# A two-block transformer kernel: output rows cleared earlier, the expert gate moved to VectorE, expert places reordered, and the closing sum made on TensorE

## The chip, the cores and the metric

The kernel runs on one core of a Trainium2 chip. A core has five engines, each with an instruction stream of its own that it works through in order: TensorE (PE, with its weight loads as PEld), VectorE (DVE), ScalarE (ACT), GpSimd (POOL) and SyncE (SP, which here only issues DMA transfers). Engines wait for one another by semaphores. The metric is the device time of one execution in microseconds (us), lower is better. The time before is 3085.83 us, the median of three runs.

## The reference

The input is 1024 tokens of width 1024, all in float32. Two blocks follow one another; the second is where most of the change lies.

```
x = first_block(x, p, ...)      # forgetting attention (16 heads), layer norm,
                                # conv-GELU FFN (2816), layer norm, gate
# second_block:
mod = silu(c) @ w_ada + b_ada
shift1, scale1, gate1, shift2, scale2, gate2 = split(mod, 6)
h   = rmsnorm(x, norm1_w) * (1 + scale1) + shift1
mix = concat(retention(h), gated_delta_rule(h)) @ w_out
x   = x + gate1 * mix
h2  = rmsnorm(x, norm2_w) * (1 + scale2) + shift2
# MoE: top-1 of 4 groups, then top-2 of the 8 experts in it; 32 experts, width 512
hid = silu(xs @ w1[e]) * (xs @ w3[e])         # xs: tokens of expert e
ys  = hid @ w2[e] * gate
x   = x + gate2 * segment_sum(ys, tok)
return rmsnorm(x, final_norm_w)
```

## The kernel before

**Precision.** A float32 product is made as three faster products. `split` (L83 to L91) writes a rounded copy `hi` (on ACT at L86, or on POOL by `pool_copy`, L80) and the rest `lo` = source − `hi` on DVE (L91); the three matmuls then stand at L108 to L110, or at L1581 for an expert's output.

**Loads.** All weight loads go through SP's one queue. `load_stage` (L150 to L154) fills one of two buffers `wst`. In the expert stage `fetch` (L1237 to L1246) takes the next of 29 buffers of 512 KB in turn (their names in the trace are `r`, `Bh`, `Bl`, `x`), so that it can run at most 29 blocks ahead of their use. An expert's weights are 12 blocks: four of `w1`, four of `w3`, four of `w2`.

**Experts.** Tokens are sorted by the number that each expert got, and the 32 experts stand in *places* of four kinds: `s` (places 0 to 2, one tile of 128 rows), `T` (3 to 6, two tiles), `M` (7 to 15, one tile of 96 or 128 rows) and `L` (16 to 31, 64 rows or fewer). `L` places use the float32 weights as they are, with no split; the other kinds split each block into a pair of parts, and `ring` (L481) holds five such pairs. `ORDER_OF` (L41) says in which order the kinds are worked. For each place POOL gathers the token rows (L1473), PE turns them (L148), `expert` (L1508 to L1590) computes, and at its end the output `y` leaves PSUM: ACT copies two halves into a `wst` buffer (L1587), POOL multiplies by the row `gate2` (`g2_row`, L1588), and POOL scatters the rows to `y_d` in DRAM by an indirect DMA (L1589). The last two places are kept on the chip by `keep` (L1592 to L1599) in the tile `both`.

**y_d.** Each token has two rows in `y_d`, one for each of its experts. Rows that no scatter writes must be zero, so POOL clears `y_d` at the start of the FFN of block 1 with two DMAs of 4 MB (L580 to L582).

**Tail.** When the experts are done, the eight tiles of 128 rows of x (`R`) and both halves of `y_d` (`Y`) are loaded (L1674, L1675). `add_rows` (L1688 to L1696) sums them: POOL adds the first `Y` to `R`, PE adds the second (through the matrix `ident`) to the kept rows (through the 0/1 matrix `oh`), DVE adds that, ACT sums squares. `scales` (L1698 to L1701) computes the norm, `finish` (L1703 to L1709) applies it and writes the output: odd tiles by ACT and POOL (L1705, L1706), even ones by DVE (L1708). `FIN` (L46) is the order of these steps (`a` add, `c` scales, `f` finish).

The order of instructions on each engine is fixed when the kernel is built, by a scheduler of the framework that works from the code's order and its own estimates.

Of the kernel before, what the change touches and what calls it, by code (L numbers as in the profile page):

```python
# [21 lines left out]
T = 1024  # L22
# [17 lines left out]

ORDER_OF = "sss" + "LLT" * 4 + "MMM" + "ML" * 6 + "LL"  # L41

GROUP = 3

RET, OUT_LAG, R_LAG = 2, 3, 2
FIN, FIN_POOL = "aaaacaaaaffffcffff", (1, 3, 5, 7)  # L46

# [78 lines left out]
def tile_kernel(ctx: ExitStack, tc: tile.TileContext, a: dict, out: bass.AP):  # L126
# [35 lines left out]
    with ph:  # L162
# [18 lines left out]
        def x_tile(t):  # L181
            xt = load_stage(x[t * 128:(t + 1) * 128, :])
            for g in range(2):
# [5 lines left out]
                split(nc, ps, xh[dst], xl[dst])  # L189

        w_in = a["attn_w_in"][0]

# [52 lines left out]
        def project(hp, begin=False):  # L245

            for i in range(2):
                kd[hp, i] = st_p.tile([128, T], F32R, name="kd")
                k66[hp, i] = st_p.tile([66, T], F32R, name="k66")
            w = load_w_cols(D + hp * 128)  # L250
            for hf in range(2):
                if hf == begin:
                    for i in range(2):
                        nc.gpsimd.dma_start(k66[hp, i][64:66, :], c_d[:, 2 * hp + i, :])
                s = slice(hf * 512, hf * 512 + 512)
                for ps in proj(w, hf):
                    yield
                for i in range(2):
                    src = ps[64 * i:64 * i + 64, :]
                    kk = kd[hp, i]  # L260
                    nc.scalar.activation(kk[0:64, s], src, AF.Copy)
                    nc.vector.tensor_tensor(k66[hp, i][0:64, s], src, kk[0:64, s], op=OP.subtract)  # L262
                    pool_copy(nc, kk[64:128, s], kk[0:64, s])
                if begin and hf == 0:
                    yield
# [263 lines left out]


    ada_d = dram.tile([6, D], F32, name="ada_d")
    ones_m = consts.tile([128, 128], F32, name="ones_m")
# [5 lines left out]
    def ada(pl):  # L538
        for j in range(6):
# [10 lines left out]
            for c in range(2):  # L550
                cs = slice(c * 512, (c + 1) * 512)
                ps = ps_g.tile([128, 512], F32, name="g")
                mm(ps, ones_m, acc[:, cs], start=True, stop=True)
                nc.vector.tensor_tensor(o_[:, cs], ps[0:1, :], b[0:1, cs], op=OP.add)
                if j in (1, 4):
# [20 lines left out]
    with tc.tile_pool(name="ffn", bufs=2, **TW) as fp:  # L576

        y_d = dram.tile([2 * T, D], F32, name="y_d")
        zero = fp.tile([128, 256], F32, name="zero", bufs=1)
        nc.gpsimd.memset(zero, 0.0)  # L580
        for k in range(2):
            nc.gpsimd.dma_start(y_d[k * T:(k + 1) * T, :].rearrange("(p t) (c f) -> p (t c) f", p=128, f=256),  # L582
                                zero[:, None, :].to_broadcast([128, 32, 256]))
        w_up = a["ffn_w_up"][0]
# [663 lines left out]
    def blocks(w1_, w3_, w2_, small):  # L1248

        up = [(w, k2) for w in (w1_, w3_) for k2 in range(4)]  # L1250
        if small:
            up = [(w, k2) for k2 in range(4) for w in (w1_, w3_)]
        return ([w[k2 * 256:(k2 + 1) * 256, :].rearrange("(k p) f -> p k f", p=128) for w, k2 in up] +
                [w2_[k * 128:(k + 1) * 128, :] for k in range(4)])
# [5 lines left out]
    with tc.tile_pool(name="mix", bufs=2, **TW) as pl:  # L1260
        wr = pl.tile([128, NK, 36], F32, name="wr", bufs=1)
        nc.sync.dma_start(wr[:, :, 0:4], a["w_group_2"][0].rearrange("(k p) f -> p k f", p=128))
        nc.sync.dma_start(wr[:, :, 4:36], a["w_expert_2"][0].rearrange("(k p) f -> p k f", p=128))
        br = pl.tile([128, 36], F32, name="br", bufs=1)
# [14 lines left out]
        def begin(t, c):  # L1279
# [5 lines left out]
            cs = slice(c * 512, (c + 1) * 512)  # L1285
            V.tensor_tensor(h2[t][:, cs], R[t][:, cs], A2[:, cs], op=OP.mult)
            nc.scalar.activation(junk, R[t][:, cs], AF.Square, scale=1.0 / 32, accum_out=ss[t][:, c:c + 1])
# [220 lines left out]
    def expert(whole, tiles, small=False, final=None, pair=None):  # L1508
# [60 lines left out]
        for n_, hT_, (_, _, dst) in zip(ns, hT, tiles):  # L1569
# [16 lines left out]
            for c in range(2):  # L1586
                nc.scalar.activation(ys[0:n_, c * 512:(c + 1) * 512], py[c], AF.Copy)  # L1587
            nc.gpsimd.tensor_tensor(ys[0:n_, :], ys[0:n_, :], g2_row[0:n_, :], op=OP.mult)  # L1588
            nc.gpsimd.indirect_dma_start(out=y_d[:, :], out_offset=bass.IndirectOffsetOnAxis(ap=dst, axis=0),  # L1589
# [82 lines left out]
    for _ in cur:  # L1672
        pass
    R = [fetch(x4_d[t * 128:(t + 1) * 128, :]) for t in range(NT)]  # L1674
    Y = [[fetch(y_d[k * T + t * 128:k * T + (t + 1) * 128, :]) for k in range(2)] for t in range(NT)]  # L1675
    fn = row(mo, a["final_norm_w_2"][None, :], "xTh", 2)
# [11 lines left out]
    def add_rows(t):  # L1688
        nc.gpsimd.tensor_tensor(R[t], R[t], Y[t][0], op=OP.add)
        for c in range(2):  # L1690
            cs = slice(c * 512, (c + 1) * 512)
            ps = ps_h.tile([128, 512], F32, name="h")
            mm(ps, ident, Y[t][1][:, cs], start=True, stop=False)
            mm(ps, oh[:, t * 128:(t + 1) * 128], both[:, cs], start=False, stop=True)
# [8 lines left out]
    def finish(t):  # L1703
        if t in FIN_POOL:
            nc.scalar.activation(R[t], R[t], AF.Copy, scale=y[:, t:t + 1])  # L1705
            nc.gpsimd.tensor_tensor(R[t], R[t], fn, op=OP.mult)  # L1706
        else:
            nc.vector.scalar_tensor_tensor(R[t], R[t], y[:, t:t + 1], fn, op0=OP.mult, op1=OP.mult)  # L1708
        nc.sync.dma_start(out[0, t * 128:(t + 1) * 128, :], R[t])  # L1709

    added = scaled = ended = 0
    for step in FIN:
# [3 lines left out]
        elif step == "c":  # L1716
            scales(scaled, added - scaled)
            scaled = added
        else:
# [30 lines left out]
```

## Time and profile before

| | |
|---|---|
| median of three runs | 3085.83 us (3080.3 to 3089.42) |
| the profiled execution | 3084.05 us, span 3082.2 us |
| TensorE's granted clock, mean over the span | 0.971 |
| PE / PEld / DVE / ACT / POOL busy | 93% / 71% / 57% / 33% / 21% |
| traffic | 440.97 MB, mean 143 GB/s |
| attention, from the start to about | 600 us |
| FFN of block 1, from about | 710 us |
| expert stage (32 places) | 2414 to 3033 us |
| tail | 3033 to 3082.2 us |

The span is what the profiler saw from the first to the last instruction; the execution's own time is 1.85 us longer. PE's 93% is a mean over stages: what a change in one stage is worth depends on what PE waits for in that stage.

### The profile page before, as it was taken

The page shows a single profiled execution, that of the slowest core. Times are in us where ns is not written, and L with a number is a line of the kernel's source. Part 1 is how long each engine was busy: PE and PEld are TensorE (multiplying, and loading weights), DVE is VectorE, ACT ScalarE, POOL GpSimd, SP SyncE. Part 2 cuts the span into 40 slices and gives each one's busy share as a digit, 9 for nine tenths or more (in the row PEclk, how much of TensorE's full clock was granted, in tenths as well). Part 3 has the DMA queues.
Part 4 walks back from the last instruction along what each step waited for, and adds up shares of the span by engine and source line. Part 5 has one row for each costly group of instructions (what it writes and reads, how often), then busy time and mean ns, then how long its engine had stood idle before and what let it go on. Part 6 is the DMA issues. An engine that isn't in the chain of part 4 may idle for free. (4 is left out here: it accounts for less than half of the span.)

```text
span 3082.2 us, 38291 instructions
## 1 busy us (share of the span) xinstructions
PE 2876.8 (93%) x13931; PEld 2175.1 (71%) x13931; DVE 1763.1 (57%) x3065; ACT 1015.0 (33%) x1773; POOL 652.7 (21%) x636
## 2 busy tenths in 40 slices
PE   7999999897999999999997999999996799999995
PEld 5777777676787877877776888888775555465542
DVE  4666666565565554555956545543568743367655
ACT  4555555512121212122224322232222333244432
POOL 2333332100000000000120022211223334444444
PEclk9999999998999999999998999999998799999998
DMA  3110111516232232332235422222556698988997
GB/s 100 34 32 29 35 36 39 185 53 194 66 116 82 82 97 69 95 96 76 102 77 96 90 72 69 78 77 71 187 162 235 234 342 315 335 306 312 382 378 286
DMA packets 276922, 440.97 MB, mean 143 GB/s; under 512 B 42698, under 2 KB 138058, under 8 KB 276604
## 3 DMA queue, kind: packets, MB, share of 16 engines
q1 hardware_dynamic: 267068, 413.28, 41.1%
q0 software_dynamic: 9664, 25.23, 2.4%
q8 instruction: 111, 1.82, 0.2%
q14 instruction: 79, 0.65, 0.1%
HBM read 382.00 MB, written 64.12 MB: 145 GB/s over the span
## 5 line engine op out<-in xcount | busy, mean ns | idle before, releaser
L108 PE MATMUL g<-Bh,hi 128*128 128x512 f32 x896 | 358.7, 401 | 6.1 <-ACT hi L86 4.9
L110 PE MATMUL g<-Bh,lo 128*128 128x512 f32 x896 | 357.2, 399 | 0.8 <-DVE lo L91 0.8
L109 PE MATMUL g<-Bl,hi 128*128 128x512 f32 x896 | 356.5, 398 | 1.2 <-DVE Bl L91 1.2
L108 PE MATMUL g<-hi,Bh 128*128 128x512 f32 x704 | 283.6, 407 | 5.9 <-ACT hi L86 5.0
L110 PE MATMUL g<-hi,Bl 128*128 128x512 f32 x704 | 283.1, 404 | 0.0
L109 PE MATMUL g<-lo,Bh 128*128 128x512 f32 x704 | 282.1, 402 | 0.5 <-DVE lo L91 0.5
L86 ACT ACTIVATE hi<-wst 128x1024 fp32r<-128x1024 f32 x122 | 128.4, 1058 | 449.2 <-PE g L110 209.9
L91 DVE TENSOR_TENSOR lo<-wst,hi 128x1024 fp32r<-128x1024 f32 x122 | 149.0, 1226 | 206.1 <-ACT hi L86 205.2
L108 PEld LDWEIGHTS g<-Bh,hi 128*128 128x128 f32 x896 | 169.6, 189 | 48.2 <-ACT hi L86 5.6
L110 PEld LDWEIGHTS g<-Bh,lo 128*128 128x128 f32 x896 | 169.6, 189 | 42.9 <-DVE lo L91 1.9
L109 PEld LDWEIGHTS g<-Bl,hi 128*128 128x128 f32 x896 | 169.4, 189 | 42.8 <-DVE Bl L91 1.7
L108 PE MATMUL g<-Bh,wh 128*128 128x512 f32 x384 | 155.3, 404 | 5.4 <-DVE k L262 3.5
L108 PEld LDWEIGHTS g<-hi,Bh 128*128 128x128 f32 x704 | 133.6, 190 | 34.8 <-ACT hi L86 6.2
L109 PE MATMUL g<-Bl,wh 128*128 128x512 f32 x384 | 155.5, 405 | 0.0
L110 PE MATMUL g<-Bh,wl 128*128 128x512 f32 x384 | 155.2, 404 | 0.0
L110 PEld LDWEIGHTS g<-hi,Bl 128*128 128x128 f32 x704 | 134.0, 190 | 29.6 <-DVE Bl L91 0.9
L109 PEld LDWEIGHTS g<-lo,Bh 128*128 128x128 f32 x704 | 133.8, 190 | 28.9 <-DVE lo L91 1.2
L621 POOL MEMSET gpad<- 128x2 f32 x22 | 2.2, 99 | 673.0 <-DVE cacc L628 672.9
L331 POOL TENSOR_SCALAR P<-P,l 128x384 f32<-128x384 f32 (+7 forms) x128 | 96.4, 757 | 223.0 <-DVE l L330 164.8
L109 PE MATMUL h<-lo,xTh 128*128 128x512 f32 (+2 forms) x320 | 130.2, 407 | 13.3 <-DVE lo L91 13.1
L109 PE MATMUL g<-lo,hh 128*128 128x512 f32 x352 | 140.2, 398 | 0.0
L108 PE MATMUL g<-hi,hh 128*128 128x512 f32 x352 | 140.1, 398 | 0.0
(542 smaller groups left out, 6351.2 us busy)
## 6 DMA issues: line engine op xcount, KB each, us to landing
r<-in_w_dram SPq DMA_DIRECT2D x107, 512.0 KB
Bh<-in_w_dram SPq DMA_DIRECT2D x105, 512.0 KB
Bl<-in_w_dram SPq DMA_DIRECT2D x104, 512.0 KB
x<-in_w_dram SPq DMA_DIRECT2D x68, 512.0 KB
wst<-in_w_ada_dram SPq DMA_DIRECT2D x48, 512.0 KB
wst<-in_ffn_w_up_dram SPq DMA_DIRECT2D x44, 512.0 KB
wst<-in_w_in_dram SPq DMA_DIRECT2D x32, 512.0 KB
wst<-in_attn_w_in_dram SPq DMA_DIRECT2D x24, 512.0 KB
```

Of the source, the lines that this page charges most:

```text
L86: nc.scalar.activation(hi, src, AF.Copy)
L91: (lo_engine or nc.vector).tensor_tensor(lo, src, hi, op=OP.subtract)
L108: nc.tensor.matmul(ps, ah, bh, start=start, stop=False, **kw)
L109: nc.tensor.matmul(ps, ah, bl, start=False, stop=False, **kw)
L110: nc.tensor.matmul(ps, al, bh, start=False, stop=stop, **kw)
L331: nc.gpsimd.tensor_scalar(p[:, :n], p[:, :n], l[:, 0:1], 1.0, op0=OP.mult, op1=OP.mult)
L621: nc.gpsimd.memset(gp[f][:, 0:2], 0.0)
```

## The change

1. **Zeros.** `y_d` and the tile `zero` are made in the attention, and `project` clears `y_d` in eight pieces of 1 MB on SP's queue. POOL's two DMAs at the start of the FFN are gone.
2. **Gate row.** DVE multiplies `y` by `g2_row` straight out of PSUM. The two ACT copies and POOL's product are gone; POOL's scatter now waits for DVE.
3. **Order of places.** `sss`, four times `LLT`, `MMM`, six times `ML`, `LL` becomes `sss`, four times `LTLM`, four times `LM`, `LLM`, `LL`.
4. **Weight rows.** A block of `w1` or `w3` holds 256 rows. Row p·2+k instead of row k·128+p now goes to partition p, so that a partition reads 4 KB in one piece instead of two pieces of 2 KB. `h2`, `shift2` and the router's weights are permuted to match (h2's 16 products read and write with stride 2; the router's weights take two DMAs more).
5. **Tail.** Loads come by tile, `Y` first; PE adds both `Y` rows; POOL adds nothing; DVE makes all the finishes; `scales` runs for two tiles at a time; `FIN` changes.

```diff
-ORDER_OF = "sss" + "LLT" * 4 + "MMM" + "ML" * 6 + "LL"
+ORDER_OF = "sss" + "LTLM" * 4 + "LM" * 4 + "LLM" + "LL"
-FIN, FIN_POOL = "aaaacaaaaffffcffff", (1, 3, 5, 7)
+FIN = "aaacaacffaacffacffff"
...
+        y_d = dram.tile([2 * T, D], F32, name="y_d")
+        zero = sm.tile([128, 256], F32, name="zero", bufs=1)
+        nc.gpsimd.memset(zero, 0.0)
+        def clear(i):
+            nc.sync.dma_start(y_d[i * 256:(i + 1) * 256, :].rearrange("(p t) (c f) -> p (t c) f", p=128, f=256),
+                              zero[:, None, :].to_broadcast([128, 8, 256]))
...
             w = load_w_cols(D + hp * 128)
+            clear(hp)
...
-        for k in range(2):
-            nc.gpsimd.dma_start(y_d[k * T:(k + 1) * T, :].rearrange("(p t) (c f) -> p (t c) f", p=128, f=256),
-                                zero[:, None, :].to_broadcast([128, 32, 256]))
...
-        return ([w[k2 * 256:(k2 + 1) * 256, :].rearrange("(k p) f -> p k f", p=128) for w, k2 in up] +
+        return ([w[k2 * 256:(k2 + 1) * 256, :].rearrange("(p k) f -> p (k f)", k=2) for w, k2 in up] +
...
-            V.tensor_tensor(h2[t][:, cs], R[t][:, cs], A2[:, cs], op=OP.mult)
+            natural = lambda z: z[:, cs].rearrange("q (a p k) -> q a k p", p=128, k=2)
+            V.tensor_tensor(in_pairs(h2[t][:, cs]), natural(R[t]), natural(A2), op=OP.mult)
...
             for c in range(2):
-                nc.scalar.activation(ys[0:n_, c * 512:(c + 1) * 512], py[c], AF.Copy)
-            nc.gpsimd.tensor_tensor(ys[0:n_, :], ys[0:n_, :], g2_row[0:n_, :], op=OP.mult)
+                cs = slice(c * 512, (c + 1) * 512)
+                nc.vector.tensor_tensor(ys[0:n_, cs], py[c], g2_row[0:n_, cs], op=OP.mult)
...
-    R = [fetch(x4_d[t * 128:(t + 1) * 128, :]) for t in range(NT)]
-    Y = [[fetch(y_d[k * T + t * 128:k * T + (t + 1) * 128, :]) for k in range(2)] for t in range(NT)]
+    R, Y = {}, {}
+    for t in range(NT):
+        Y[t] = [fetch(y_d[k * T + t * 128:k * T + (t + 1) * 128, :]) for k in range(2)]
+        R[t] = fetch(x4_d[t * 128:(t + 1) * 128, :])
...
-        nc.gpsimd.tensor_tensor(R[t], R[t], Y[t][0], op=OP.add)
         for c in range(2):
...
-            mm(ps, ident, Y[t][1][:, cs], start=True, stop=False)
+            for k in range(2):
+                mm(ps, ident, Y[t][k][:, cs], start=(k == 0), stop=False)
             mm(ps, oh[:, t * 128:(t + 1) * 128], both[:, cs], start=False, stop=True)
```

On SP, at the start of the program, the loads of x and of the first weights stood like this (`wst<-in_x_dram` is a tile of x, `wst<-in_attn_w_in_dram` a block of attention weights):

```order
L152 DMA wst<-in_x_dram 128x1024 x2
L217 DMA bf_c<-in_attn_b_f_dram 16x1
L535 DMA c_col<-in_c_dram 128x8x1
L212 DMA P<-in_attn_w_in_dram 128x8x16
L152 DMA wst<-in_x_dram 128x1024 x2
L152 DMA wst<-in_attn_w_in_dram 128x8x128
L152 DMA wst<-in_x_dram 128x1024 x4
L152 DMA wst<-in_attn_w_in_dram 128x8x128 x4
```

The code calls one clear for each pair of heads, but the scheduler has put all eight (L197) between these first loads:

```order
L197 DMA y_d<-zero 1024x1x256
L152 DMA wst<-in_x_dram 128x1024 x2
L221 DMA P<-in_attn_w_in_dram 128x8x16
L197 DMA y_d<-zero 1024x1x256
L152 DMA wst<-in_attn_w_in_dram 128x8x128
L152 DMA wst<-in_x_dram 128x1024
L197 DMA y_d<-zero 1024x1x256
L152 DMA wst<-in_x_dram 128x1024
L197 DMA y_d<-zero 1024x1x256 x2
L152 DMA wst<-in_x_dram 128x1024 x2
L197 DMA y_d<-zero 1024x1x256
L152 DMA wst<-in_attn_w_in_dram 128x8x128 x2
```

Two clears stand ahead of the first block of attention weights, and three more ahead of the last two tiles of x.

On DVE, around the end of the first `s` place, the `lo` parts of the weights and of the turned rows (`hTl`, `xTl`) stood like this:

```order
L91 TENSOR_TENSOR hTl<-t,hTh 128x512
L91 TENSOR_TENSOR xTl<-t,xTh 128x512
L91 TENSOR_TENSOR lo<-Bl_18422,hi 128x1024 x2
L91 TENSOR_TENSOR lo<-r_18750,hi 128x1024
L91 TENSOR_TENSOR lo<-Bh_18780,hi 128x1024
L91 TENSOR_TENSOR xTl<-t,xTh 128x512
L91 TENSOR_TENSOR lo<-Bh_18780,hi 128x1024 x2
```

Now the two products by the gate row (L1603) stand in that row, among the `lo` parts of the next place's weights:

```order
L91 TENSOR_TENSOR hTl<-t,hTh 128x512
L91 TENSOR_TENSOR xTl<-t,xTh 128x512
L91 TENSOR_TENSOR lo<-Bl_18430,hi 128x1024 x2
L91 TENSOR_TENSOR lo<-r_18758,hi 128x1024
L91 TENSOR_TENSOR lo<-Bh_18788,hi 128x1024
L1603 TENSOR_TENSOR wst<-y,g_row 128x512 x2
L91 TENSOR_TENSOR xTl<-t,xTh 128x512
L91 TENSOR_TENSOR lo<-Bh_18788,hi 128x1024 x2
```

Three `lo` parts of the next place stand behind a wait for this place's last product.

On PE, at the start of the tail, half a tile took two matmuls:

```order
L1575 MATMUL y<-Bh_18421,hTh 32x512 x2
L1693 MATMUL h<-r_24083,ident 128x512
L1694 MATMUL h<-xTl 128x512
L1693 MATMUL h<-r_24083,ident 128x512
L1694 MATMUL h<-xTl 128x512
```

It now takes three, two of them through `ident`:

```order
L1590 MATMUL y<-Bh_18429,hTh 32x512 x2
L1710 MATMUL h<-Bh_18429,ident 128x512 x3
L1711 MATMUL h<-xTl 128x512
L1710 MATMUL h<-Bh_18429,ident 128x512
L1711 MATMUL h<-xTl 128x512
```

One `ident` matmul for each of the 16 half tiles has been added. Between the attention and the expert stage the engines' orders are otherwise as before.

## Rows read from the trace of the kernel before

**Rows 1.** Busy times by stretch: us, each engine busy (instructions), PEclk, DMA share, GB/s

```profile
0.00:45.00 45.00, 33.70 (x150) 24.74 (x151) 19.02 (x28) 19.11 (x29) 3.60 (x13) 1.00 0.50 142
722.00:737.00 15.00, 0.89 (x4) 0.38 (x2) 0.18 (x1) 1.26 (x2) 0.00 (x0) 0.68 1.03 355
737.00:745.00 8.00, 6.30 (x20) 5.25 (x21) 4.12 (x6) 2.44 (x5) 0.00 (x0) 0.53 0.86 219
2414.00:2484.00 70.00, 64.78 (x280) 47.72 (x278) 55.85 (x47) 35.30 (x45) 27.67 (x19) 0.95 0.80 271
2484.00:2741.00 257.00, 249.55 (x1153) 140.79 (x1152) 96.54 (x92) 82.74 (x131) 100.95 (x65) 0.99 0.91 330
2741.00:2813.00 72.00, 62.64 (x260) 45.80 (x259) 61.23 (x49) 33.77 (x43) 34.50 (x23) 0.95 0.88 297
2813.00:2971.00 158.00, 151.69 (x715) 78.69 (x713) 98.13 (x82) 64.68 (x96) 72.37 (x48) 1.00 1.00 362
2971.00:3011.00 40.00, 35.09 (x148) 15.81 (x148) 16.02 (x13) 12.18 (x21) 13.16 (x9) 0.91 1.03 382
3011.00:3033.00 22.00, 19.71 (x96) 5.36 (x92) 4.79 (x7) 4.07 (x8) 3.24 (x2) 1.00 1.01 398
```

**Rows 2.** Timeline at the start of the FFN: start us, us, engine, line, operation

```profile
710.82 3.46 POOL L582 DMA_DIRECT2D y_d<-zero  x2 [0.24 <-POOL gpad L621]
...
735.74 1.06 ACT L86 ACTIVATE hi<-wst 128x1024 fp32r<-128x1024 f32 x1 [21.25 <-DMA wst<-in_ffn_w_up_dram]
```

**Rows 3.** Timeline at the program's start

```profile
15.76 13.71 SPq L152 DMA_DIRECT2D wst<-in_x_dram  x4
...
17.58 0.79 PE L108 MATMUL g<-Bh,wh 128*128 128x512 f32 x1 [1.85 <-ACT wh L86]
```

**Rows 4.** Timeline of POOL and DVE in the stretch of three M places

```profile
2767.66 2.43 POOL L1588 TENSOR_TENSOR wst<-wst,g_row 128x1024 f32<-128x1024 f32 x1
2767.69 4.50 DVE L91 TENSOR_TENSOR lo<-Bl,hi 128x1024 fp32r<-128x1024 f32 x1 [0.24 <-ACT hi L86]
...
2784.82 1.23 DVE L91 TENSOR_TENSOR lo<-r,hi 128x1024 fp32r<-128x1024 f32 x1 [0.80 <-ACT hi L86]
```

**Rows 5.** The lo tiles alone, busy over the expert stage: PE, PEld, DVE, POOL

```profile
2414.00:3033.00 619.00, 182.17 (x480) 84.45 (x480) 272.35 (x187) 0.00 (x0) 0.98 0.93 333
```

**Rows 6.** Timeline of POOL in the last ML pair

```profile
2991.69 0.99 POOL L1678 IOTA xg<- 128x1024 f32 x1 [11.39 <-PE t L148]
```

**Rows 7.** Instructions by line: count, ns min/median/max, first and last start

```profile
L1597 DVE TENSOR_TENSOR wst<-y,g_row x4: 680/682/686, 3022.2 to 3034.0; 32x512 f32<-32x512 f32 x4
L1587 ACT ACTIVATE wst<-y x68: 579/592/600, 2439.4 to 3011.5; 128x512 f32<-128x512 f32 x22, 64x512 f32<-64x512 f32 x16, 96x512 f32<-96x512 f32 x14, 48x512 f32<-48x512 f32 x12
L1589 POOL DMA_INDIRECT y_d<-wst,tabI x34: 894/1675/2007, 2445.6 to 3014.8; - x34
L1286 DVE TENSOR_TENSOR h<-r,A x16: 680/690/694, 2287.4 to 2371.8; 128x512 f32<-128x512 f32 x16
```

**Rows 8.** The tail: chain that ended last, and timeline

```profile
3041.45 0.86 PE h L1693 x2
3042.31 0.23 PE h L1694
...
3046.96 0.70 DVE Bh L1695
...
3067.07 0.16 DVE L103 SCALAR_TENSOR_TENSOR rms_y<-fin_t,rms_y 128x4 f32<-128x4 f32 x1
3067.27 1.28 DVE L1708 SCALAR_TENSOR_TENSOR Bl<-Bl,rms_y,xTh 128x1024 f32<-128x1024 f32 x1
...
3074.14 0.33 SPq L1709 DMA_DIRECT2D out_dram<-Bl  x1
```

**Rows 9.** DVE by line and by form ahead of the experts

```profile
L1389 DVE TENSOR_TENSOR sel<-OH,slots 128x256 f32<-128x256 f32 x2 | 1.1, 613 | 0.0
L1386 DVE TENSOR_TENSOR slots<-slots,wrap 128x256 f32<-128x256 f32 x1 | 0.4, 403 | 0.0
```

More of the change, by code (lines that the diff above doesn't have):

```diff
@@ L528, in tile_kernel, with in_pairs @@
                 turn_in(ps_t, R[t], t)
+    def in_pairs(z):
+        return z.rearrange("q (a k p) -> q a k p", k=2, p=128)
     ada_d = dram.tile([6, D], F32, name="ada_d")
@@ L553, in ada @@
                 mm(ps, ones_m, acc[:, cs], start=True, stop=True)
+                if j == 3:
+                    nc.vector.tensor_tensor(in_pairs(o_[:, cs]), ps[0:1, :].rearrange("o (a p k) -> o a k p", a=2, k=2),
+                                            b[0:1, cs].rearrange("o (a p k) -> o a k p", a=2, k=2), op=OP.add)
+                    continue
                 nc.vector.tensor_tensor(o_[:, cs], ps[0:1, :], b[0:1, cs], op=OP.add)
@@ L576, in tile_kernel @@
     with tc.tile_pool(name="ffn", bufs=2, **TW) as fp:
-        y_d = dram.tile([2 * T, D], F32, name="y_d")
-        zero = fp.tile([128, 256], F32, name="zero", bufs=1)
-        nc.gpsimd.memset(zero, 0.0)
-        for k in range(2):
-            nc.gpsimd.dma_start(y_d[k * T:(k + 1) * T, :].rearrange("(p t) (c f) -> p (t c) f", p=128, f=256),
-                                zero[:, None, :].to_broadcast([128, 32, 256]))
         w_up = a["ffn_w_up"][0]
@@ L1261, in tile_kernel @@
         wr = pl.tile([128, NK, 36], F32, name="wr", bufs=1)
-        nc.sync.dma_start(wr[:, :, 0:4], a["w_group_2"][0].rearrange("(k p) f -> p k f", p=128))
-        nc.sync.dma_start(wr[:, :, 4:36], a["w_expert_2"][0].rearrange("(k p) f -> p k f", p=128))
+        for k in range(2):
+            wr_k = wr.rearrange("p (a k) f -> p a k f", k=2)[:, :, k, :]
+            nc.sync.dma_start(wr_k[:, :, 0:4], a["w_group_2"][0].rearrange("(a p k) f -> p a k f", p=128, k=2)[:, :, k, :])
+            nc.sync.dma_start(wr_k[:, :, 4:36], a["w_expert_2"][0].rearrange("(a p k) f -> p a k f", p=128, k=2)[:, :, k, :])
         br = pl.tile([128, 36], F32, name="br", bufs=1)
@@ L1692, in add_rows @@
             ps = ps_h.tile([128, 512], F32, name="h")
-            mm(ps, ident, Y[t][1][:, cs], start=True, stop=False)
+            for k in range(2):
+                mm(ps, ident, Y[t][k][:, cs], start=(k == 0), stop=False)
             mm(ps, oh[:, t * 128:(t + 1) * 128], both[:, cs], start=False, stop=True)
@@ L1703, in finish @@
     def finish(t):
[L1704 to L1708, printed above, removed]
+        nc.vector.scalar_tensor_tensor(R[t], R[t], y[:, t:t + 1], fn, op0=OP.mult, op1=OP.mult)
         nc.sync.dma_start(out[0, t * 128:(t + 1) * 128, :], R[t])
@@ L1716, in tile_kernel @@
         elif step == "c":
-            scales(scaled, added - scaled)
-            scaled = added
+            scales(scaled, 2)
+            scaled += 2
         else:
```

## The prediction

> **What bounds the kernel now.** I began with the engines' shares. TensorE is busy for 93% of the span, so the most that any change can give back is what TensorE idles, plus the time that it runs at its lower clock, plus work taken off it. The change takes nothing off TensorE and adds matmuls in the tail. So I asked, stretch by stretch, where TensorE idles and why; the borders of the stretches in [rows 1] are the ends of a place's last product.
>
> *Start.* In the first 45 us the DMA engines are half busy and TensorE works for 33.7 us. SP's four last loads of x take it 13.71 us from 15.76 on, and the first product with weights starts at 17.58 [rows 3].
>
> *FFN.* POOL issues both clears at 710.82. From 722 to 737 the transfers are at a share of 1.03 and TensorE works for 0.89 of 15 us; for the 8 us after that it is granted 0.53 of its clock [rows 1]. ACT waits 21.25 us for a block of `w_up` and goes on at 735.74 [rows 2]. The weights stand behind 8 MB of zeros: at 355 GB/s the 8.4 million bytes take 23.6 us, which is the length of the hole.
>
> *Experts.* In 619 us, TensorE idles 5.2 us in the three `s` places (2414 to 2484), 7.5 in four times `LLT`, 9.4 in `MMM`, 6.3 in the first five `ML` pairs, 4.9 in the last, 2.3 in the last two `L` places: 35.5 in all [rows 1]. The three `M` places in a row take 72 us, 24 each. A pair `ML` takes 158/5 = 31.6, and an `L` 22/2 = 11, so an `M` beside an `L` takes 20.6. In `MMM` DVE is busy for 61 of 72 us: a `lo` that takes 1.23 us alone takes 4.50 while POOL multiplies by the gate row [rows 4]. All 187 `lo` operations take 272 us where 187 × 1.23 = 230 would do [rows 5], so 42 us of DVE's time is lengthening, of which I put about half on POOL's product. The last `ML` pair takes 40 us: POOL stands 11.39 us at an iota of the tail, ahead of `hi` copies that TensorE needs [rows 6].
>
> *Tail.* 49.2 us from 3033.0 to 3082.2.
>
> **The change, part by part.**
>
> *Zeros at the start: +4.* Eight transfers of 1.05 MB, by the 355 GB/s of [rows 1] 3.0 us each. Two stand ahead of the first weight block on the same queue; the first falls into a gap in which SP waits for a buffer, so one counts: +3. Three more stand among the last four loads of x: 4 × 0.52 MB are 5.9 us of the 13.71, the other 7.8 are idle, and 9.0 of clears go in: +1.2. The last three delay weight blocks that are wanted later. If the idle transfer time (share 0.50 of 45 us) covers all, 0; if none of it, +24. I take 4, nearer the cover, since 22.5 us of idle share stand against 23.6.
>
> *FFN: −17.* The 14.1 us in which TensorE idles from 722 to 737, and of the 8 us at 0.53 the lost 0.47 × 8 = 3.8: −17.9. What is late next is the block's small convolution weights behind the same loads; for that I leave 1 us. Range −12 to −18.
>
> *Order of places: −18.6.* The three `M` leave their row: 3 × (24 − 20.6) = −10.2. In the new order TensorE turns the rows in the buffer that the iota overwrites before it comes to the last `M`'s output, so that the stall should go and the last pair take 31.6 in place of 40: −8.4. The four `T` keep an `L` on both sides.
>
> *Gate row: −4.* Before, `y` left by two ACT copies of 0.59 us, POOL's 2.43 and the scatter of 1.68 [rows 4, 7]; now by two DVE products and the scatter. The product exists in the trace for 32 rows, at 0.68 us [rows 7], and other 512-wide DVE operations on 128 rows cost 0.69. So a chain is 2.2 us shorter, and there are 34. That can give back no more than TensorE idles in `s` and `LLT`, 12.7 us [rows 1]; the ends are 0 and −12.7, I take the middle, −6. In return DVE gets 34 × 1.38 = 47 us of work, and loses perhaps half of the 42 us of lengthened `lo`. DVE is busy for 333 of the 619 us, so there is room, except in `s` (55.85 of 70), where two or three of them may show: +2. The ends are 0 and, if nothing hides them, +47 (a rival below). The DVE product now waits at DVE's head for TensorE, with two or three `lo` of the next place behind it; TensorE waits for those once its five pairs of parts are used up.
>
> The parts for the experts sum to −22.6, with a range from 0 to −33 (all idle time but the last 2.3).
>
> *Weight rows: 0.* The stretch in which two thirds of the blocks' rows are 2 KB reaches 382 GB/s at a share of 1.03, and the last, which holds mostly 4 KB rows, 398 [rows 1]: 4%. Where TensorE sets the pace (151.69 of 158 us) it gives nothing; if transfers do, −8. *h2 with stride 2: 0.* The trace has a stride of 32 bytes: 613 against 403 ns, 1.5 times as long [rows 9]. On 16 products of 0.69 us [rows 7] that is at most +5.6; 8 bytes is nearer to contiguous 4 than to 32, so I take nothing. The Trainium skill, "SBUF — State Buffer", section "Door 1: The DMA port swizzle", says that accesses run at full rate as long as two or more of them fall into one 16-byte line. By it a stride of 8 bytes costs nothing, and the 613 ns agree with it, since each access there has a line of its own; a stride of 8 stands in no row.
>
> *Tail: +3.4.* TensorE now has two `ident` matmuls and one `oh` for a half tile: 0.86 + 0.86 + 0.23 = 1.95 us [rows 8], 16 of them 31.2. Behind the last come half a us of waiting and DVE's add of 0.70. The scheduler has put six finishes of about 1.2 us, the small operations (12 of 0.2) and two more finishes behind the last add on DVE: 7.2 + 2.4 + 2.4. From the last output's issue at 3074.14 to the end it was 8.1 us. In all 52.5 against 49.2: +3.4. It is 0 if the loads and the adds run ahead of TensorE's last product, and +8 if each finish waits for the tail's loads of R, which came before the experts' end until now.
>
> Sum: 4 − 17 − 22.6 + 0 + 0 + 3.4 = −32.2 on the profiled execution's 3084.05: 3051.9. The median of the runs is 1.8 us above that execution, well inside the range. Forecast 3052.
>
> **Rivals.**
>
> *Transfers set the pace from 2813 on.* For it: shares of 1.00 to 1.03 in all three stretches [rows 1], and the end of the new order has denser weight traffic (four `LM`, then `LLM`, then `LL`). Against it: 0.80 to 0.91 in the stretches before, which a faster start can use. Then the expert stage stays at 619 us: 3084.05 + 4 − 17 + 3.4 = 3074.5. The Trainium skill, "DMA: Bandwidth & Descriptors", section "Where 436 GB/s comes from", has the memory side bind at about 358 GB/s for a core. By that the stage from 2813 on would already stand at its limit, and this rival would be the likeliest; the 382 and 398 of [rows 1] are above it, so I don't take it as a limit.
>
> *The clears are paid in full.* For it: all eight stand in the first 45 us on the queue that feeds TensorE, and at the FFN such a queue cost its whole length. Against it: half of the transfer time there was idle. +20 in place of +4, with a little less gained: 3071.
>
> *DVE is the new bound (slower).* The gate products wait at DVE's head for TensorE's last `y`, the `lo` parts behind them come late, and TensorE waits at the next place. If all 47 us come onto TensorE's path, and none of the lengthening of `lo` goes away, the time is 3051.9 + 47 − 2 = 3096.9. It passes no change at 32 us, 0.95 us for each of the 34 evictions, and is slower by over 0.3% from 41 us on. Against it: DVE is busy for just over half of the stage, and five pairs of parts are ready ahead.
>
> *More comes back.* All idle time of TensorE from 2414 to 3011 goes (33 us in place of 22.6): 3041.
>
> *The change does nothing at the FFN:* the hole of 722 to 737 might be the loads' own. The row of 8.4 MB against 23.6 us speaks so plainly against it that I leave it inside the range.
>
> **How the numbers follow.** Forecast 0.62; transfers 0.14; clears in full 0.10; more comes back 0.09; DVE the bound 0.05. The measurement can tell about 0.3%, 9.3 us, so no change is 3076.6 to 3095.1. Of the forecast's 0.62 some 0.03, and of the two rivals at 3071 and 3074.5 some 0.05, reach above 3076.6: faster 0.87, same 0.08, slower 0.05. Low end: −18 at the FFN and −33 in the experts with nothing lost at the start and in the tail gives 3033. High end: the transfers' 3074.5 and 2 us of what the tail can cost: 3077. All mechanisms but one are of one sign.
>
> **What would show it right or wrong.** The zeros: no POOL DMA at the FFN's start, ACT's wait for `w_up` under 3 us instead of 21.25, the clock at its higher level there; and TensorE's first product with weights at 20 to 22 us. The order: no `M` beside an `M`, an `M` of some 20.6 us, the expert stage at about 596 us. The gate row: `lo` at a mean near 1.3 us, DVE's product at 0.69, and no wait of TensorE for `lo` of more than 1 us a place. The weight rows: GB/s above 382 at a share of 1. The tail: 51 to 54 us, TensorE idle for little of its first 31. The prediction is wrong if the start's products are late by more than 10 us, if the stage stays above 610 us at a transfer share of 1, or if DVE's products stand waiting while TensorE waits for `lo`.

## The result, and the profile after

| | median of runs | profiled execution | ratio to before, 95% interval |
|---|---|---|---|
| before | 3086.26 us | 3084.05 us | |
| changed | 3029.77 us (3027.43 to 3031.5) | 3031.5 us | 0.9819, 0.9802 to 0.9836 |

The kernel became 56 us faster. The direction was forecast; the time lies below the range (3033 to 3077), 22 us under the 3052 predicted. I lined up the two traces by equal TensorE instructions. The changed kernel is 3.3 us ahead at 73 us, 3.8 ahead of the FFN's hole, 22.1 at the start of the FFN's second product, 21.7 at the first expert; it gains 29.5 in the experts (619.6 to 590.1) and 1.2 in the tail (49.0 to 47.8).

Busy times by stretch, in the columns of [rows 1]. First the stretch of the start that changed most, before and after:

```profile
42.00:56.00 14.00, 10.45 (x40) 8.09 (x39) 7.39 (x7) 7.37 (x9) 7.96 (x6) 0.85 0.16 42
...
42.00:56.00 14.00, 14.00 (x62) 11.25 (x61) 9.32 (x10) 7.63 (x10) 5.48 (x5) 1.00 0.62 196
```

Then the changed kernel; the last six lines are the `s` places, four times `LTLM`, four times `LM`, `LLM`, `LL` and the tail:

```profile
722.00:737.00 15.00, 15.00 (x66) 12.06 (x65) 9.30 (x12) 4.93 (x7) 0.00 (x0) 1.00 0.64 141
737.00:745.00 8.00, 8.00 (x36) 6.40 (x35) 5.15 (x6) 2.16 (x3) 0.00 (x0) 1.00 0.65 200
...
2391.90:2458.80 66.90, 64.71 (x278) 49.12 (x279) 54.12 (x55) 34.61 (x41) 24.21 (x17) 0.94 0.78 285
2458.80:2779.10 320.30, 320.24 (x1491) 194.01 (x1490) 178.20 (x193) 104.59 (x144) 87.15 (x72) 1.00 0.90 341
2779.10:2908.80 129.70, 125.71 (x578) 65.81 (x578) 76.82 (x81) 42.33 (x62) 42.90 (x32) 0.97 1.01 382
2908.80:2957.80 49.00, 46.47 (x209) 20.14 (x210) 22.75 (x25) 12.38 (x20) 12.29 (x9) 0.97 1.02 399
2957.80:2982.00 24.20, 21.91 (x95) 5.82 (x96) 5.87 (x9) 3.00 (x6) 0.93 (x1) 0.93 0.89 349
2982.00:3029.80 47.80, 31.35 (x80) 14.99 (x80) 30.45 (x76) 10.45 (x18) 0.00 (x0) 0.88 0.61 243
```

For 320 us of `LTLM` TensorE idles 0.06 us. The hole and the low clock at the FFN [rows 1, 2] are gone. For the block that ACT waited 21.25 us for, it now waits 6.23, more than the 3 that the prediction allowed, but TensorE is busy meanwhile:

```profile
716.33 1.06 ACT L86 ACTIVATE hi<-wst 128x1024 fp32r<-128x1024 f32 x1 [6.23 <-DMA wst<-in_ffn_w_up_dram]
```

The `lo` tiles alone over the expert stage, which answer to [rows 5]: 187 `lo` in 234 us in place of 272, so 39 of the 42 us of lengthening went.

```profile
2391.90:2981.96 590.06, 181.56 (x480) 84.42 (x480) 233.71 (x187) 0.00 (x0) 0.98 0.92 349
```

DVE's product out of PSUM and h2's product with stride 2, by line:

```profile
L1603 DVE TENSOR_TENSOR wst<-y,g_row x68: 672/683/694, 2419.8 to 2958.2; 128x512 f32<-128x512 f32 x22, 64x512 f32<-64x512 f32 x16, 96x512 f32<-96x512 f32 x14, 48x512 f32<-48x512 f32 x12
...
L1301 DVE TENSOR_TENSOR h<-r,A x16: 683/689/694, 2266.3 to 2350.0; 128x512 f32<-128x512 f32 x16
```

The view that I had not read is TensorE's own waits over the expert stage (who it waited for, us in all, times, longest; the 8.5 us for SP end where the stage begins). Before:

```profile
PE h L109 <- DVE lo L91: 13.1, 12, 1.9
PE t L148 <- SPq L1627: 8.5, 1, 8.5
PE t L148 <- DVE hid L1529: 8.2, 5, 2.3
PE t L148 <- DVE hid L1549: 6.5, 7, 1.4
```

After:

```profile
PE t L148 <- SPq L1642: 8.5, 1, 8.5
PE h L108 <- ACT hi L86: 3.2, 4, 1.3
PE h L109 <- DVE lo L91: 2.8, 4, 1.0
PE t L148 <- DVE hid L1544: 1.5, 1, 1.5
```

So 28 us of waits for `lo` and `hid`, in short pieces all over the stage, became 4. One piece of them, from the timeline of before (POOL, DVE, TensorE):

```profile
2548.98 2.40 POOL L1588 TENSOR_TENSOR wst<-wst,g_row 128x1024 f32<-128x1024 f32 x1
2551.35 2.01 POOL L80 TENSOR_SCALAR hi<-r 128x1024 fp32r<-128x1024 f32 x1
...
2553.40 1.23 DVE L91 TENSOR_TENSOR lo<-r,hi 128x1024 fp32r<-128x1024 f32 x1 [0.94 <-POOL hi L80]
2554.54 0.73 DVE L1529 SCALAR_TENSOR_TENSOR hid<-h,tabG,hid 64x512 f32<-64x512 f32 x1
...
2555.33 0.46 PE L148 MATMUL t<-ident,hid 64*128 64x64 f32 x4 [1.62 <-DVE hid L1529]
```

Read it from the end: TensorE waits 1.62 us to turn `hid`. `hid`, the hidden rows of an expert, stands on DVE behind a `lo` of another place's weights; that `lo` waits for its `hi`; the `hi` stands on POOL behind the product by the gate row. A product that nobody on TensorE needs soon holds up, over two in-order rows, one that TensorE needs now. In the changed kernel DVE waits only for ACT at such a place:

```profile
2510.30 2.35 DVE L91 TENSOR_TENSOR lo<-Bh,hi 128x1024 fp32r<-128x1024 f32 x2
2514.05 0.74 DVE L1544 SCALAR_TENSOR_TENSOR hid<-h,tabG,hid 64x512 f32<-64x512 f32 x1 [1.40 <-ACT hid L1543]
```

### The profile page after: what moved, and what is told of

Its sections match the earlier page's. It is cut to its first block, busy times and chain, and to the rows that moved or that the text cites. A ratio compares the mean times of both kernels' runs of the same rounds, so it can differ in the third digit from the quotient of the medians.

```text
span 3029.8 us, 38345 instructions
## 1 busy us (share of the span) xinstructions
PE 2880.3 (95%) x13963; PEld 2178.8 (72%) x13963; DVE 1769.6 (58%) x3161; ACT 975.9 (32%) x1701; POOL 535.3 (18%) x588
## 5 line engine op out<-in xcount | busy, mean ns | idle before, releaser
L110 PE MATMUL g<-hi,hl 128*128 128x512 f32 x352 | 138.2, 393 | 0.0
```

Of the source, the lines that this page charges most:

```text
L110: nc.tensor.matmul(ps, al, bh, start=False, stop=stop, **kw)
```

## Experiments

Ratios are to the kernel before on the same chip, with their 95% interval; "stage" is the expert stage of the profiled run, 619.6 us before and 590.1 changed; the runs below that keep the changed order and eviction have stages of 585 to 590 us, so that a few us of a stage tell nothing.

**The parts undone one by one.** The zeros as before:

```diff
-            clear(hp)
...
+        for k in range(2):
+            nc.gpsimd.dma_start(y_d[k * T:(k + 1) * T, :].rearrange("(p t) (c f) -> p (t c) f", p=128, f=256),
+                                zero[:, None, :].to_broadcast([128, 32, 256]))
...
```

> The changed kernel, with y_d cleared by POOL at the start of the FFN again, as before. Theory (the zeros are worth what the two traces' alignment shows, -3.4 us up to 70 us and -18.3 at the FFN): 3029.8 + 21.7 = 3051 us, with ACT's wait of some 20 us for w_up back, and in the first 100 us the lull of 3.5 us on TensorE and the granted clock of 0.85 from 42 to 56 us back too, since the clears on SP's queue are what moved the first instructions. Rival (the start's gain has another cause, and the clears alone cost the 3 us by which the first product with weights came later): the FFN's +18 less 3 at the start, 3045 us, with no lull in the first 100 us.

3051.49 us, ratio 0.9883 (0.9866 to 0.9899): 22 us, the theory's value. ACT's wait came back (21.50 us), and at the start so did the lull, row for row (the line of before is above); lined up with the trace of before, this one is within 0.2 us of it at 73 us and behind the FFN's hole.

```profile
42.00:56.00 14.00, 10.46 (x39) 8.06 (x38) 7.39 (x7) 7.22 (x9) 8.10 (x6) 0.84 0.16 42
```

The order of places as before:

```diff
-ORDER_OF = "sss" + "LTLM" * 4 + "LM" * 4 + "LLM" + "LL"
+ORDER_OF = "sss" + "LLT" * 4 + "MMM" + "ML" * 6 + "LL"
```

> The changed kernel with the old order of places (sss, LLT four times, MMM, ML six times, LL). Theory of the prediction (three Ms in a row cost 10.2 us and the last pair's stall 8.4, whatever evicts): 3029.8 + 18.6 = 3048 us, an M in MMM at some 24 us. Rival (an M in a row was slow because POOL's gate product lengthened lo; with that gone the order matters little): an M in MMM at 20 to 21 us, 3036 us or less.

3031.55 us, 0.9821 (0.9804 to 0.9837), stage 586.6: no different, with the three `M` at 20.4 each. My theory falls, and the rival holds.

The eviction as before:

```diff
-                nc.vector.tensor_tensor(ys[0:n_, cs], py[c], g2_row[0:n_, cs], op=OP.mult)
+                nc.scalar.activation(ys[0:n_, c * 512:(c + 1) * 512], py[c], AF.Copy)
+            nc.gpsimd.tensor_tensor(ys[0:n_, :], ys[0:n_, :], g2_row[0:n_, :], op=OP.mult)
```

> The changed kernel with the old eviction (two ACT copies, POOL's product by the gate row). Theory of the prediction (the gate row on DVE is worth 4 us): 3034 us. Rival (it is worth far more, since each pair ML got 1.2 us shorter and lo 39 us shorter in all): 3040 us or more, with lo at a sum of some 270 us over the expert stage and pairs LM at 31.5 us.

3067.76 us, 0.9937 (0.9919 to 0.9954), stage 623.1: this part is worth 38 us in the changed kernel. The rival holds.

The weight rows as before, and with them h2, shift2 and the router's weights:

```diff
-        return ([w[k2 * 256:(k2 + 1) * 256, :].rearrange("(p k) f -> p (k f)", k=2) for w, k2 in up] +
+        return ([w[k2 * 256:(k2 + 1) * 256, :].rearrange("(k p) f -> p k f", p=128) for w, k2 in up] +
...
```

> The changed kernel with the old layout of w1 and w3 (two pieces of 2 KB), of h2, shift2 and the router's weights. Theory of the prediction (neither the pieces nor the stride matter): 3030 us, within 3. Rival (transfers set the pace in the last 233 us of the expert stage, where they stand at a share of 1.00 to 1.02, so that the pieces' 4 per cent come back there): 3038 us, at a lower GB/s at the same share.

3029.36 us, 0.9813 (0.9797 to 0.9829): nothing, as predicted. At a share of 1.03 the loads reach 375 and 382 GB/s where the changed kernel has 382 and 399; TensorE loses nothing by it.

**The two disputed parts alone,** put into the kernel before. The eviction (the diff above, reversed):

> The kernel before with the new eviction alone. Theory (the eviction carries the expert stage's whole gain, whatever the order): 3086 - 30 = 3056 us, with Ms in MMM at 20 to 21 us. Rival (order and eviction each give a part and only together the whole): 3065 to 3080 us.

3057.80 us, 0.9914 (0.9896 to 0.9931): 27 us, the theory's value. Here the stage and its three `M` in a row, at 20.4 each:

```profile
2412.70:2999.20 586.50, 573.22 (x2640) 332.73 (x2640) 339.77 (x359) 196.64 (x273) 172.74 (x131) 0.99 0.96 348
2726.90:2788.00 61.10, 56.81 (x255) 43.52 (x254) 55.75 (x54) 30.78 (x38) 28.24 (x19) 1.00 0.96 334
```

The stage is 33.1 us shorter, more than the whole change gave there, and 33.0 is also what the old eviction costs the changed kernel (623.1 against 590.1). Alone it brings 27 because the tail gives 6.5 back, 55.5 us in place of 49.0 (below). TensorE's idle time in it fell by 22, and its busy time, for the same matmuls, from 584.0 to 573.2, at a mean granted clock of 0.99 in place of 0.98 [rows 5]: where short idle pieces went, some of the lower clock went with them.

The order alone:

> The kernel before with the new order of places alone. Theory of the prediction (the order is worth 18.6 us): 3067 us. Rival (with the old eviction as with the new one the order is worth about nothing; in the runs with old and new order under the new eviction the expert stage took 586.6 and 590.1 us): 3083 to 3090 us.

3084.05 us, 1.0001 (0.9992 to 1.0011): nothing, as the rival said. Inside, the profiled run is not the same: its stage is 7 us longer (626.6) and its tail 6 us shorter (43.1).

**What in the eviction costs.** DVE copies out of PSUM, POOL multiplies:

```diff
-                nc.vector.tensor_tensor(ys[0:n_, cs], py[c], g2_row[0:n_, cs], op=OP.mult)
+                nc.vector.tensor_copy(ys[0:n_, cs], py[c])
+            nc.gpsimd.tensor_tensor(ys[0:n_, :], ys[0:n_, :], g2_row[0:n_, :], op=OP.mult)
```

> The changed kernel, in which DVE only copies the two halves of y out of PSUM and POOL multiplies by the gate row, as it did before. DVE has as much to do as in the changed kernel; only POOL's product of two tiles is put back. Theory (POOL's product lengthens DVE's lo beside it, and DVE's row comes late): some 3060 us, between 3055 and 3068, with the lo of the expert stage at some 270 us in all in place of 234 and TensorE waiting some 20 us for DVE's lo and hid. Rival (the old eviction was slow since ACT's copies, in ACT's row, came late; POOL's product is beside TensorE's path): 3030 to 3038 us.

3056.84 us, 0.9906 (0.9889 to 0.9924), as the theory said: 27 of the 38 us come back with POOL's product.

The changed kernel's eviction, with two copies on POOL ahead of the scatter:

```diff
+            for _ in range(2):
+                pool_copy(nc, ys[0:n_, :], ys[0:n_, :])
```

> The changed kernel, with two copies of the evicted tile onto itself on POOL ahead of the scatter, each with one tile read (1.1 us each, 2.2 to 2.4 in all: as long as the product by the gate row, and on the same place of POOL's row). Theory (two operands read by POOL are what lengthens lo): lo stays at some 234 us in all, and the time at 3030 to 3036 us. Rival (any work of POOL of this length does it, by holding back the hi copies behind it or by contention): 3050 us or more.

3040.87 us, 0.9858 (0.9842 to 0.9875), between the two, and the reason given for the theory is wrong: copies that read one tile lengthen `lo` about as much in sum (264.5 us, the second line) as the product does (267.7, the first):

```profile
2393.90:3008.50 614.60, 182.57 (x480) 84.28 (x480) 267.67 (x187) 0.00 (x0) 0.98 0.89 334
...
2390.90:2990.80 599.90, 181.42 (x480) 84.63 (x480) 264.53 (x187) 0.00 (x0) 0.98 0.91 343
```

ACT copies, DVE multiplies from the copied tile:

```diff
-                nc.vector.tensor_tensor(ys[0:n_, cs], py[c], g2_row[0:n_, cs], op=OP.mult)
+                nc.scalar.activation(ys[0:n_, c * 512:(c + 1) * 512], py[c], AF.Copy)
+            nc.vector.tensor_tensor(ys[0:n_, :], ys[0:n_, :], g2_row[0:n_, :], op=OP.mult)
```

> The changed kernel with ACT's two copies out of PSUM as before, and the product by the gate row made by DVE from the copied tile in place of POOL. The chain from the last product to the scatter is as long as before less 1.1 us, and POOL has nothing to do in it. Theory (POOL's product is the cause): 3030 to 3036 us. Rival (the length of the chain or ACT's part in it is the cause): 3050 us or more.

3043.24 us, 0.9866 (0.9849 to 0.9883), with `lo` at 229.7 and no product on POOL: 13 us, which neither number foresaw. DVE stands 96.3 us in all at the product until ACT has copied, and TensorE waits for `hid` again:

```profile
PE t L148 <- DVE hid L1564: 10.4, 8, 1.5
```

So a part of the 38 comes without POOL. It is no fixed price of the longer chain: the run with one constant, below, keeps ACT's copies too, and its stage is as short as with the new eviction.

POOL's product cut into four:

```diff
+            for c in range(4):
+                cs = slice(c * 256, (c + 1) * 256)
+                nc.gpsimd.tensor_tensor(ys[0:n_, cs], ys[0:n_, cs], g2_row[0:n_, cs], op=OP.mult)
```

> The changed kernel with DVE's copies out of PSUM and POOL's product by the gate row, as in the run with POOL's product, but cut into four products of 256 columns. Theory (a single lo is held for up to 3.8 us beside the long product and for 2.6 beside short copies, and the longest hold is what costs 16 us more than the two copies do): 3041 to 3046 us, with no lo over 2.6 us. Rival (the time that POOL reads two operands is what costs): 3053 to 3062 us, as with the one product.

3074.30 us, 0.9965 (0.9953 to 0.9978): both were wrong, and it settles much. The `lo` tiles and TensorE's waits of this run:

```profile
2392.70:3023.70 631.00, 184.12 (x480) 85.10 (x480) 250.50 (x187) 0.00 (x0) 0.97 0.88 327
```

```profile
PE h L109 <- DVE lo L91: 11.4, 12, 1.6
PE t L148 <- DVE hid L1564: 10.6, 7, 3.3
...
PE h L108 <- POOL hi L80: 4.9, 5, 1.5
```

`lo` is lengthened least of the runs with added work on POOL (250.5), the time is the longest. What grew is POOL's own row: the four parts take 129.6 us in all, the one product 85.9. So it is not the lengthening of `lo`, in sum, that sets the time.

**POOL's `hi` copies given to ACT**, in the kernel before, with the product left where it was:

```diff
-HI_POOL = (2, 5, 8, 11)
+HI_POOL = ()
```

> The kernel before, with the hi copies of the experts' weights that POOL made (one in three) made by ACT like the others; the gate row stays with ACT and POOL. Theory (what costs is POOL's row: its product holds back the hi copies behind it, their lo wait in DVE's row, and hid stands behind those): with no hi behind the product, TensorE's wait for DVE's hid and lo falls from 28 us to under 12 and the time to 3065 us or less, though POOL's product still stands beside DVE's lo. Rival (the lengthening of lo beside the product is what costs): 3078 us or more, with lo still at some 260 us in all.

3056.81 us, 0.9908 (0.9889 to 0.9927), stage 587.8. One constant gives what the new eviction gives, 27 us, and the theory holds. The same two views:

```profile
2414.00:3001.80 587.80, 180.02 (x480) 83.64 (x480) 255.32 (x187) 0.00 (x0) 0.99 0.96 349
```

```profile
PE h L109 <- DVE lo L91: 4.6, 6, 2.1
...
PE t L148 <- DVE hid L1529: 2.5, 3, 1.5
PE t L148 <- DVE hid L1549: 1.4, 4, 0.4
```

`lo` is still lengthened (255 us), the waits for `lo` and `hid` fell from 28 to 8.5. So it was through the `hi` copies on POOL's row, not through `lo`'s own length, that the product cost.

The same edit in the changed kernel:

> The changed kernel with the same edit. Theory (with the product gone there is little left to hold back on POOL's row, and ACT's row gets 66 us more with waits in it): 3030 us, within 6. Rival (POOL's hi copies still come late behind gathers and scatters that wait): 3022 us or less.

3023.95 us, 0.9808 (0.9791 to 0.9825): at the edge of the theory's range, and not to be told from the changed kernel by the interval; the `s` places took 63.3 us in place of 66.9. So POOL's `hi` copies cost 27 us where the product stands ahead of them, and some 6, if anything, where it does not.

**Tail and rows.** The old tail in the changed kernel (loads, `add_rows`, `scales`, `finish` and `FIN` as before):

```diff
-FIN = "aaacaacffaacffaacffff"
+FIN, FIN_POOL = "aaaacaaaaffffcffff", (1, 3, 5, 7)
...
+        nc.gpsimd.tensor_tensor(R[t], R[t], Y[t][0], op=OP.add)
...
```

> The changed kernel with the old tail: R loaded ahead of Y, POOL adds the first Y and makes half of the finishes. Theory of the prediction (the new tail costs 3.4 us, since TensorE's matmuls set its pace): 3026 us. Rival (the new tail is faster: in the run with the new eviction alone, the old tail took 55.5 us from the last product to the end, and the new one takes 47.8): 3037 us, with POOL's adds and products, at 2.8 us and more each, on the chain that ends last.

3028.90 us, 0.9828 (0.9811 to 0.9845), a tail of 47.2 us: no difference that can be told. The rival falls; the theory's 3026 lies inside the interval, but the tail is 0.6 us shorter, not 3.4. Then old rows and old tail together, both diffs above:

> The changed kernel with both the old weight rows and the old tail. Theory (the tail took 55.5 us with the new eviction alone, because the old rows and the old tail together leave the tail's loads late, and either new one mends it): a tail of some 55 us, 3036 us. Rival (the old order of places is what leaves them late): a tail of some 47 us, 3029 us.

3040.36 us, 0.9855 (0.9838 to 0.9872), a tail of 53.1: near the theory. And the old order's diff with these two, which leaves the zeros and the eviction:

> The changed kernel with the old order, the old weight rows and the old tail, so that only the zeros and the eviction are new. Theory (the two parts add up, -28 for the eviction alone and -22 for the zeros, and the tail's loads are late as with the eviction alone): 3036 us with a tail of some 55 us. Rival (the other three parts are worth nothing even together): 3030 us.

3040.22 us, 0.9855 (0.9836 to 0.9874), a tail of 53.1 again. So rows and tail are worth some 10 us together and nothing singly. SP's last loads for the tail in the run with both old, and in the changed kernel:

```profile
2996.27 4.15 SPq L1253 DMA_DIRECT2D x<-y_d  x4
```

```profile
2991.35 0.32 SPq L1257 DMA_DIRECT2D x<-x_d  x1
```

Counted from the last expert's product (2985.31 and 2981.96), the last load is issued 14.8 us after it with the old rows and 9.4 with the new. The new tail works tile by tile as they come and hides that: with the old rows and the new tail the last load is issued 16.7 us after the product, and the tail still takes 47.9. In the old tail POOL's eight adds go one after another as the `Y` land; the last starts 23.8 us after the product with the old rows and 17.4 with the new.

**Other orders.** The changed kernel with its halves exchanged:

```diff
-ORDER_OF = "sss" + "LTLM" * 4 + "LM" * 4 + "LLM" + "LL"
+ORDER_OF = "sss" + "LM" * 4 + "LLM" + "LTLM" * 4 + "LL"
```

> The changed kernel with the two halves of its order exchanged: sss, LM four times, LLM, LTLM four times, LL. The same places, but those that want most bytes for their time stand where the 29 blocks loaded ahead are full, and those that want least at the end. Theory (the two Ms of 26 and 24 us near the end, against 17 us elsewhere, are slow because transfers, at a share of 1.01 there, don't keep up): no M over 20 us, 3015 us. Rival (they are slow for another reason, such as the order in which the tail's and the last places' small operations stand on ACT and POOL): the Ms in the middle as fast as any and the last M still slow, 3022 to 3035 us.

3025.70 us, 0.9813 (0.9795 to 0.9831), stage 583.5: not to be told from the changed kernel. The time is the rival's, but neither account holds: the slow `M` (23.8 us) now stands in the middle, in `LLM`, and the last `M` takes 17.9. With the odd `L` ahead of a `T`:

```diff
-ORDER_OF = "sss" + "LTLM" * 4 + "LM" * 4 + "LLM" + "LL"
+ORDER_OF = "sss" + "LM" * 5 + "LTLM" * 3 + "LLTLM" + "LL"
```

> The changed kernel in another order: sss, LM five times, LTLM three times, LLTLM, LL. The one L too many stands ahead of a T in place of ahead of an M. Theory (an M behind two Ls takes 24 us in place of 17 wherever it stands, a T behind two Ls loses nothing): an expert stage of 577 us in place of 583.5 in the swapped order, no M over 20 us, 3019 us. Rival (the place behind two Ls costs a T as much as an M): 3026 us.

3027.95 us, 0.9813 (0.9793 to 0.9833), an `M` of 24.2 us that stands behind one `L`: the theory falls, and why one `M` is slow stays open. What the slow `M` of 26 us in the changed kernel is made of can be read:

```profile
2882.60:2908.80 26.20, 22.57 (x86) 12.64 (x88) 15.51 (x15) 8.44 (x12) 8.40 (x6) 0.87 1.01 375
```

TensorE idles 3.6 us of it, 2.1 of them for the first block's `hi` and `lo`, and its granted clock is 0.87: from 2885.5 to 2891.6, right behind that wait, matmuls follow one another at 0.43 us in place of 0.23, the lower of its two levels.

Last, the exchanged order and `HI_POOL = ()` together, both diffs above:

> The changed kernel with all the experts' hi copies on ACT and the two halves of its order exchanged. Theory (both edits take away waits in different places: in the three s places, and at the M that came late near the end): 3020 us, an expert stage of 577 to 580 us. Rival (each already takes the same few us): 3024 us, a stage of 583.

3019.18 us (3017.4 to 3020.14), 0.9784 (0.9771 to 0.9798), stage 576.6, as the theory said. It beats both kernels; its interval lies below the changed kernel's.

## Why the prediction was wrong, step by step

The sum came out 20 us short (−32.2 against −52.6 of the profiled executions): start 7, expert stage 7, tail 5, FFN 1. The stage's −22.6 against −29.5 looks near by luck: its two terms, −18.6 and −4, measured about 0 and −33. The range's low end, 3033, held the FFN (−18) and the stage (−33), and both stayed inside; it gave the start and the tail nothing, and they gave 3.3 and 1.2 us.

- **FFN, −17:** right; 18.3 by the traces.
- **Start, +4:** the first product with weights came at 19.92 us, 2.3 later, near what was said. But the clears also moved the first instructions: a lull of 3.5 us and a clock of 0.85 went, and 3.3 us remained as a gain. Mis-sized by 7: the step counted what the clears take on the queue, with 0 as its best end, and not what they do to the order behind them.
- **Gate row, −4: the step that failed.** It measured 33 us of the stage, alone and in the changed kernel (27 and 38 us of the time). Two sentences failed: "That can give back no more than TensorE idles in `s` and `LLT`, 12.7 us" set the cap by stretches, and so gave the idle time of `MMM` and the last pair to another cause before asking what TensorE waited for there; and the cap counted idle time alone, though the 0.95 and 0.91 of the clock stood in the same rows [rows 1]. What the product cost was TensorE's waits for `lo` and `hid`, 28 us, over POOL's and DVE's rows. The prediction named the lengthened `lo` [rows 4, 5], and most of that did go, but it was a companion: with `lo` at 255 us the time came back all the same, once no `hi` stood behind the product. And the 4.50 us of [rows 4] were read as the product's alone; POOL's next line belongs to them:

```profile
2770.03 1.07 POOL L80 TENSOR_SCALAR hi<-r 128x1024 fp32r<-128x1024 f32 x1
```

That `lo` started with the product at 2767.7 and ended at 2772.2, 1.1 us after this copy: it seems to have stood through both.

- **Order, −18.6: failed.** 0 alone. Counted between the last products of places, the three `M` did fall in the run with the order alone, from 72.2 us to 60.1, but the `L` and `T` that stand there took 9 us more: an `M` was priced by its new neighbours, and what it does to them was left out. With POOL's product gone, an `M` in `MMM` takes 20.4 anyway. The stall at the iota was read as TensorE's; but in that `M` TensorE waited 2.2 us for ACT's `hi` and 2.4 for `lo`, and the last `M` takes 26.5 us with no `hi` on POOL at all, and 24.2 in the new order.
- **Weight rows, 0:** right for this kernel; they bring the tail's loads 5 to 7 us forward, which shows only with the old tail. **h2, 0:** right, 689 ns against 690. Only its two reads have the stride; the result is written contiguously. The Trainium skill's rule ("SBUF — State Buffer", "Door 1: The DMA port swizzle") holds here for reads at a stride of 8 bytes.
- **Tail, +3.4:** measured −1.2. TensorE's 31.35 us are as worked out. Mis-sized was the end, taken as 8.1 us from the last output's issue; here the last add, the last finishes and the last outputs:

```profile
3013.39 0.69 DVE L1712 TENSOR_TENSOR x<-x,h 128x512 f32<-128x512 f32 x1 [0.40 <-PE h L1711]
...
3023.27 2.48 DVE L1721 SCALAR_TENSOR_TENSOR x<-x,rms_y,xTh 128x1024 f32<-128x1024 f32 x2
```

```profile
3024.59 1.53 SPq L1722 DMA_DIRECT2D out_dram<-x  x2
```

The second of the two outputs is issued at 3025.8, when its finish is done; from there to the end, 3029.8, it is 4.0 us. The 8.1 belonged to the old tail: in all seven runs that have it, the end comes 8.0 to 8.1 us after POOL's last product, 5.7 to 5.9 after the last output has landed. With the new tail, in which POOL has nothing to do, it comes 1.6 to 1.7 after the landing. What takes that time the traces don't show.

- **Rivals:** DVE did stand at its products, 74 us in all, waiting for TensorE's `y`, but TensorE waited only 2.8 us for `lo`. "More comes back" was the nearest: TensorE idles 24.6 us less in the stage, and for the same matmuls it is busy 5 us less. The clears were not paid at all, and the FFN's hole was theirs. That transfers bound is not shown: from 2779 to 2958 us they stand at a share of 1.01 and 1.02, at up to 399 GB/s, and TensorE idles 6.5 us, but its waits there name `hi` and `lo`, no block. The Trainium skill's 358 GB/s for a core ("DMA: Bandwidth & Descriptors", "Where 436 GB/s comes from") is passed here as it was before.

Left open: why POOL's product costs 16 us more than two copies that hold POOL as long (TensorE's waits for `lo` and `hid` are 24 against 16 us), why the slow `M`'s first `hi` and `lo` come late, and what the clears moved at the start so that the lull went.

## What to carry to other kernels

List the waits of the engine that bounds the kernel, over the whole stage, before costing an edit, and follow each back through the in-order rows; a short wait that comes at many places is not seen stretch by stretch. An instruction that nobody needs soon is dear where one that is needed stands behind it, however idle its engine is. Give idle time to a cause only after undoing that cause alone.

## What was not expected of the hardware

In no run were DVE's operations that read PSUM lengthened (the product by the gate row 0.70 us at most, `hid` 0.75), while `lo`, which reads two tiles from SBUF, took up to 2.8 us beside POOL copies that read one tile and up to 4.6 beside its products, and 1.27 at most in the two runs where POOL made neither. It goes both ways: a product of 256 columns on POOL took 0.74 us in the median and 4.63 at most. And in the seven runs whose tail ends with a product on POOL, the end of the span came 4 us later behind the last landing than in the others (5.7 to 5.9 us in place of 1.6 to 1.7).
